# Background work paced by VectorE time, chains one step per block, and the centre tap of a short convolution on ACT

## The chip, the cores and the metric

One core of one Trainium2 chip. The metric is the device time of one execution in microseconds, lower is better. Engines are called PE (TensorE), DVE or VectorE, ACT (ScalarE), POOL (GpSimd) and SP (SyncE, which here only issues DMAs).

## The reference, cut to what matters

Two groups, each of 2048 tokens of width 1024, go through the same layer in float32:

```python
h = rmsnorm(x, norm_g)
p = h @ w_in                                   # 1024 -> 3328 columns
hy_u, hy_z, cf_a, cf_z, xa_q, xa_z = split(p)
k2   = hyena_two_sided_filter(...)             # 3 sine layers, times exp decay: (2L, 512)
u    = depthwise_conv(hy_u, width 3) + b;  x0, x1, v = split(u)
y_hy = x0 * bidir_fftconv(v * x1, k2, skip) * silu(hy_z)
y_cf = silu(layernorm(depthwise_conv(val * sigmoid(gate), width 31))) * silu(cf_z)
y_xa = memory_attention(xa_q, rmsnorm(mem), w_kv) * silu(xa_z)
x    = x + concat(y_hy, y_cf, y_xa) @ w_out;   y = rmsnorm(x)
```

## The kernel before

The run has four phases in time: the start (0 to 76 us), the projection `p = h @ w_in` (to about 1390), the FFT and attention stages (to about 1740) and the output projection. The change touches the projection only.

There the 3328 columns are cut into 26 tiles of 128, the tokens of a group into four blocks of 512 (`tb`). One **block** is one column tile for 512 tokens: `proj` (L402) issues 24 matmuls into one of two PSUM tiles "pj", three for each of eight k-steps, since every operand is split into a high and a low part (`split`, L176: a cast on ACT, a subtraction on POOL or VectorE). There are 104 blocks per group, 208 in all; I number them 1 to 208 in program order. The list `seq` (L632 to L641) sets the order of columns: conformer gate and value (cg, cv), conformer output gate (zc), the pairs x1 and v of the Hyena branch, the pairs of its gate zh and x0, and the attention's zx and q. The last entry of group 0 runs zx1 and q1 together, token block by token block (blocks 97 to 104), since each time group 0's x for a token block is done with, `build_xt` puts group 1's in its place.

After its matmuls a block has an epilogue. For x0, x1 and v that is `hy_conv` (L416): ACT copies the PSUM tile to SBUF (L423), POOL makes the centre tap with the bias (L430), VectorE adds the two outer taps (L432, L434), and `gate` multiplies on POOL (L451).

**Background work** is cut into steps kept in two queues, `bgq` and `fq`. After each block `background(BR, FR)` (L626) takes up to seven steps of `bgq` and one of `fq`, whatever they cost; not after blocks 97 to 104. What is in the queues, and after which column (`QUEUE`, L621; `n` counts columns of a group):

- `kv_background` (L523): keys and values of the memory, ten steps and two `store`s, taken at blocks 9 and 10.
- `cf_background(g)` (L209): the width-31 convolution and layer norm of the conformer, for four token blocks b. Each has two `start`s (a load and the first tap on POOL), 60 taps on VectorE (`tap`, L218) and then `center`, `var`, `norm`, `fin`, `outp`. `mean` (L223) adds two tiles on POOL, splits the sum and has PE add over channels by a matmul with ones (L227, L228). Group 0's is queued before block 25 and taken until block 63, group 1's is taken at blocks 125 to 163.
- `filter_background` (L271): the Hyena filter, 32 `taps` steps in eight groups b of four, each group after three `mlp` layers that follow on one another: a matmul (L294), then VectorE, POOL, VectorE, POOL, and a Sin on ACT (L305, L308). A `taps` step has three matmuls (L320 to L322), an Exp on ACT (L324), a product on VectorE (L325), a matmul with the Fourier matrix (L332), a copy on ACT (L333) and a store. It's queued at group 1's first column.
- `a_background` (L584): the first Fourier step of eight of the channels' pieces, queued late in group 1.

`load_x(1, tb)` (L369) brings in group 1's x, in two halves of 256 tokens: `normed` (L347) loads four pieces, each into a "bg" tile, for the sum of squares (L354), puts 1/rms on a diagonal in the first of these tiles (L363), spreads it over the partitions by two matmuls into an "ms" tile `r` (L364), and scales the half (L366). Then `build_xt` (L378) splits it (L385, L386). `load_x(1, 0)` is issued two columns before group 1, the other three inside the last entry of group 0.

**Tiles** are taken from pools by tag: "bg" has six (NBT; a conformer block holds four of them, `hb` and `acc` for two channels, and two more for the halves of each mean), "ms" is four PSUM tiles for all the background's matmuls and `r`, "big" three, "sm" six, "f512" two and "f256" three. A request waits until a tile is released. The order of instructions on each engine is laid out ahead of time from the program by a scheduler; work may stand earlier on its engine than where the program issues it. At the end `bg(len(bgq))` empties the queues.

Of the kernel before, what the change touches and what calls it, by code (L numbers as in the profile page):

```python
# [15 lines left out]
ALU = mybir.AluOpType  # L16
# [86 lines left out]
def kernel(ctx: ExitStack, tc: tile.TileContext, a: dict):  # L103
    nc = tc.nc
    LEAD, BR, FR, PF = 8, 7, 1.0, 0
# [53 lines left out]

    bgq, fq = deque(), deque()  # L160

    def bg(n, q=bgq):
        for _ in range(min(n, len(q))):
            q.popleft()()
# [23 lines left out]
    with ExitStack() as c1:  # L188
# [20 lines left out]
        def cf_background(g):  # L209
# [13 lines left out]
            def mean(src, tmp):  # L223
                mp, hi, lo = ms(), bt(TB, F32R), bt(TB, F32R)
                nc.gpsimd.tensor_tensor(tmp, src[0], src[1], op=ALU.add)
                split(hi, lo, tmp)
                nc.tensor.matmul(mp, ones, hi, start=True, stop=False)  # L227
                nc.tensor.matmul(mp, ones, lo, start=False, stop=True)  # L228
                return mp

            def center(st):
                mp = mean([st["a", c] for c in range(2)], st["h", 0][:, 0:TB])
                for c in range(2):
                    nc.vector.tensor_tensor(st["a", c], st["a", c], mp, op=ALU.subtract)

            def var(st):
# [3 lines left out]
                vp = mean([st["q", c] for c in range(2)], st["q", 1])  # L240
                nc.scalar.activation(st["q", 0], vp, AF.Sqrt, bias=eps)

            def norm(st):
                nc.vector.reciprocal(st["q", 0], st["q", 0])

            def fin(st, c):
                acc = st["a", c]
                nc.gpsimd.tensor_tensor(acc, acc, st["q", 0], op=ALU.mult)
                nc.scalar.activation(acc, acc, AF.Silu, bias=vb[:, 66 + c:67 + c], scale=vb[:, 64 + c:65 + c])

            def outp(st, b, c):
                z = st["q", 1 - c]
                nc.sync.dma_start(z, SZ[g][c][:, b * TB:(b + 1) * TB])
                acc = st["a", c]
                nc.gpsimd.tensor_tensor(acc, acc, z, op=ALU.mult)
                nc.sync.dma_start(YN[g][c][:, b * TB:(b + 1) * TB], acc)

            for b in range(NB):
                st = {}
                for c in range(2):  # L260
                    bgq.append(lambda st=st, b=b, c=c: start(st, b, c))
                for k in range(1, CK):
                    for c in range(2):
                        bgq.append(lambda st=st, c=c, k=k: tap(st, c, k))
                for f in (center, var, norm):
                    bgq.append(lambda st=st, f=f: f(st))
                bgq.append(lambda st=st, b=b: (fin(st, 0), fin(st, 1)))
                bgq.append(lambda st=st, b=b: (outp(st, b, 0), outp(st, b, 1)))


        def filter_background():  # L271
# [42 lines left out]
            def taps(st, b, n):  # L314
                n2p = b * 4 + n
                if n % 2 == 0:
                    st["tf"] = ft(W)
                    nc.sync.dma_start(st["tf"], a["tf"][:, n2p:n2p + 2, :].rearrange("p n k -> p (n k)"))
# [672 lines left out]
```

## Time and profile before

| | us |
|---|---|
| median of 3 runs | 2164.81 (2164.49 to 2169.85) |
| profiled execution | 2161.23 |
| its span | 2159.5 |
| PE busy in the span | 2009.7 (93%) |
| VectorE busy | 1297.8 (60%) |
| ACT busy | 807.3 (37%) |
| POOL busy | 1015.1 (47%) |
| mean granted TensorE clock | 0.978 |

PE works nearly all the time, so what isn't PE's work shows as a gap on PE or as a lower granted clock (1.00 stands for the upper of its two levels, 2.4 GHz, 0.50 for the lower, 1.2 GHz). The mean shares of the other engines hide that they differ by stretch: VectorE is over 90% busy in some and under 50% in others. So the profile is best read by stretches of the projection phase.

### The profile page before, as it was taken

To read this page: it belongs to the slowest core of one execution; us is meant where nothing else is said; L and a number is where in the kernel's file an instruction comes from. 1 tells how busy PE (TensorE), PEld (TensorE's weight loads), DVE (VectorE), ACT (ScalarE), POOL (GpSimd) and SP (SyncE) were. 2 spreads that over 40 slices of the span, in tenths; PEclk is the share of its full clock that TensorE was granted. 3 is DMA by queue.
4 is the path that set the end of the run, shared out by engine and by line. 5 is a ranking of instruction groups with operands and counts; after the bars stand their busy time and mean duration, and the time that the engine had idled before them with its cause. 6 is when DMAs were issued, how large, how long until landed. Compare 5 with 4: busy or idle time off the path is not lost.

```text
span 2159.5 us, 26758 instructions
## 1 busy us (share of the span) xinstructions
PE 2009.7 (93%) x9186; PEld 1604.0 (74%) x9186; DVE 1297.8 (60%) x1781; ACT 807.3 (37%) x1625; POOL 1015.1 (47%) x1015
## 2 busy tenths in 40 slices
PE   5999998898999999989989899999998889999998
PEld 5888876776787888877768687789732278888886
DVE  6664497977336473489494953287887724434443
ACT  5431212132524333322424244387787712111211
POOL 3434576576534323486565752364588811111110
PEclk9999999999999999999999999999999999999999
DMA  8541111121546222111212226798688785655552
GB/s 305 171 152 54 59 49 63 55 69 45 195 152 193 71 72 77 65 66 59 70 66 73 75 84 195 215 297 268 187 258 269 239 197 150 154 152 143 151 153 56
DMA packets 175842, 293.05 MB, mean 136 GB/s; under 512 B 50665, under 2 KB 71801, under 8 KB 172890
## 3 DMA queue, kind: packets, MB, share of 16 engines
q1 hardware_dynamic: 148474, 232.20, 35.3%
q10 hardware_dynamic: 21392, 46.18, 6.5%
q0 software_dynamic: 5840, 12.95, 2.2%
q8 instruction: 73, 1.20, 0.2%
q14 instruction: 63, 0.52, 0.1%
HBM read 186.87 MB, written 104.39 MB: 135 GB/s over the span
## 4 chain that ended last, share of the span: by engine, by line
PE 63%; DVE 16%; issue 6%; DMA 6%; POOL 4%; ACT 3%; SPq 1%; ACTq 0%; POOLq 0%; DVEq 0%
PE pj L410 11%; PE pj L409 11%; PE pj L411 11%; DVE bg L219 8%; PE ms L936 5%; PE ms L938 5%; PE ms L937 5%; PE tr L919 2%; PE po L760 2%; DVE sm L432 1%; DVE big L366 1%; DMA big<-in_xt_dram 1%; PE ms L739 1%; PE ms L332 1%; PE ms L546 1%
## 5 line engine op out<-in xcount | busy, mean ns | idle before, releaser
L409 PE MATMUL pj<-xh,whi 128*128 128x512 f32 (+1 forms) x1728 | 672.9, 390 | 24.2 <-ACT sm L423 6.6
L410 PE MATMUL pj<-xl,whi 128*128 128x512 f32 (+1 forms) x1728 | 671.6, 389 | 9.2 <-POOL xl L386 7.8
L411 PE MATMUL pj<-xh,wlo 128*128 128x512 f32 (+1 forms) x1728 | 670.4, 388 | 0.0
L219 DVE SCALAR_TENSOR_TENSOR bg<-bg,vb,bg 128x512 f32<-128x512 f32 x480 | 428.0, 924 | 10.7 <-POOL bg L214 5.9
L409 PEld LDWEIGHTS pj<-xh,whi 128*128 128x128 f32 x1728 | 332.0, 192 | 93.9 <-ACT sm L423 7.8
L410 PEld LDWEIGHTS pj<-xl,whi 128*128 128x128 f32 x1728 | 332.2, 192 | 74.1 <-POOL xl L386 8.7
L411 PEld LDWEIGHTS pj<-xh,wlo 128*128 128x128 f32 x1728 | 332.0, 192 | 64.6
L178 POOL TENSOR_TENSOR wlo<-sm,whi 128x256 fp32r<-128x256 f32 x204 | 190.5, 959 | 89.5 <-ACT whi L177 86.3
L936 PE MATMUL ms<-wo,mh 128*128 128x512 f32 x512 | 206.7, 404 | 1.8 <-ACT mh L177 1.8
L937 PE MATMUL ms<-wo,mh 128*128 128x512 f32 x512 | 201.3, 393 | 0.0
L938 PE MATMUL ms<-wo,ml 128*128 128x512 f32 x512 | 198.9, 395 | 0.2 <-POOL ml L178 0.2
L432 DVE SCALAR_TENSOR_TENSOR sm<-sm,va,sm 128x448 f32<-128x448 f32 (+1 forms) x96 | 82.7, 861 | 161.9 <-POOL sm L430 136.7
L939 DVE TENSOR_TENSOR xr<-xr,ms 128x512 f32<-128x512 f32 x64 | 44.0, 688 | 203.7 <-PE ms L938 203.7
L184 POOL TENSOR_TENSOR ss<-ss,mhalf 128x1 f32<-128x1 f32 x32 | 17.6, 550 | 315.9 <-DVE ss L183 315.9
L430 POOL TENSOR_SCALAR sm<-sm,va 128x448 f32<-128x448 f32 (+1 forms) x96 | 113.5, 1182 | 102.2 <-ACT sm L423 82.2
L451 POOL TENSOR_TENSOR big<-big,sm 128x448 f32<-128x448 f32 (+1 forms) x64 | 118.6, 1853 | 77.7 <-DVE sm L434 70.8
L182 ACT ACTIVATE junk<-xr 128x1024 bf16<-128x1024 f32 x32 | 33.8, 1058 | 318.4 <-DVE xr L939 318.2
L423 ACT COPY sm<-pj 128x512 f32<-128x512 f32 x96 | 56.0, 585 | 199.6 <-PE pj L411 150.1
L177 ACT CAST whi<-sm 128x256 fp32r<-128x256 f32 x208 | 73.0, 404 | 139.4 <-DMA sm<-in_win_dram 106.4
L936 PEld LDWEIGHTS ms<-wo,mh 128*128 128x128 f32 x512 | 97.2, 190 | 20.5 <-ACT mh L177 2.6
L938 PEld LDWEIGHTS ms<-wo,ml 128*128 128x128 f32 x512 | 96.4, 188 | 20.9 <-POOL ml L178 0.6
L937 PEld LDWEIGHTS ms<-wo,mh 128*128 128x128 f32 x512 | 97.2, 190 | 19.0
(179 smaller groups left out, 3096.9 us busy)
## 6 DMA issues: line engine op xcount, KB each, us to landing
sm<-in_win_dram SPq DMA_DIRECT2D x104, 256.0 KB, 3.4
big<-in_xt_dram SPq DMA_DIRECT2D x32, 512.0 KB, 5.9
in<-x1d SPq DMA_DIRECT2D x128, 128.0 KB, 3.3
aa<-o ACTq DMA_DIRECT2D x64, 256.0 KB, 3.6
at<-aa SPq DMA_DIRECT2D x64, 256.0 KB, 4.1
out_dram<-xr ACTq DMA_DIRECT2D x64, 256.0 KB, 3.3
x1d<-us ACTq DMA_DIRECT2D x48, 256.0 KB, 4.5
in<-xf SPq DMA_DIRECT2D x66, 128.0 KB, 3.7
```

Of the source, the lines that this page charges most:

```text
L177: nc.scalar.copy(hi, src)
L178: (sub_eng or nc.gpsimd).tensor_tensor(lo, src, hi.bitcast(F32), op=ALU.subtract)
L219: nc.vector.scalar_tensor_tensor(st["a", c], st["h", c][:, k:k + TB], vb[:, 2 * k + c:2 * k + c + 1], st["a", c], op0=ALU.mult, op1=ALU.add)
L409: nc.tensor.matmul(ps[:, ts_], hi, xh[:, k, ts_], start=k == 0, stop=False)
L410: nc.tensor.matmul(ps[:, ts_], hi, xl[:, k, ts_], start=False, stop=False)
L411: nc.tensor.matmul(ps[:, ts_], lo, xh[:, k, ts_], start=False, stop=k == KC - 1)
L430: nc.gpsimd.tensor_scalar(ct[:, o:e], pt[:, o + 1:e + 1], w[1], va[:, 52 + ch:53 + ch], op0=ALU.mult, op1=ALU.add)
L432: nc.vector.scalar_tensor_tensor(ct[:, o:e], pt[:, o:e], w[0], ct[:, o:e], op0=ALU.mult, op1=ALU.add)
L451: nc.gpsimd.tensor_tensor(v, v, out, op=ALU.mult)
L936: nc.tensor.matmul(po, mh[:, k, :], woh[k][:, hs], start=i == 0, stop=False)
L937: nc.tensor.matmul(po, mh[:, k, :], wol[k][:, hs], start=False, stop=False)
L938: nc.tensor.matmul(po, ml[:, k, :], woh[k][:, hs], start=False, stop=i == 7)
```

## The change

Each background step now carries a cost in us of VectorE and a flag "chain". After each block, `background(us)` gets a credit of 5.0 less the column's own VectorE cost (`own`: 2.2 for x0, x1 and v, 0.8 for cv and q, 0.1 for others) and takes steps while credit is left, `fq` before `bgq`, but at most one chain step of each queue per block. A tap costs 0.9 and is no chain step.

- The conformer's steps are cut anew: the sum and split of a mean stand at the end of one step, its matmul at the head of the next; per token block `start`, 60 taps, `total`, `center`, `var`, `outp`.
- The filter's `taps` loses its second half, which becomes `spec`, done one step later; a step is now `spec` of the tap step before, `taps`, and in 21 of 32 steps an `mlp` layer of the next group. It's queued at column 12 of group 0 (taken from block 57) instead of at group 1's first.
- `kv_background` and `a_background` are chain steps; the two `mult`s of an `a_background` piece become one step.
- In `hy_conv` the centre tap goes from POOL to ACT.

```diff
+    pace = {"block": 0, "credit": 0.0, "last": {id(bgq): -1, id(fq): -1}}
+    def background(us):
+        pace["block"] += 1
+        pace["credit"] = min(pace["credit"], us) + us
+        chained = set()
+        while pace["credit"] > 0:
+            for q in (fq, bgq):
+                if not q:
+                    continue
+                cost, chain, fn = q[0]
+                if chain and (id(q) in chained or pace["last"][id(q)] == pace["block"]):
+                    continue
+                if chain:
+                    chained.add(id(q))
+                q.popleft()
+                fn()
+                pace["last"][id(q)] = pace["block"]
+                pace["credit"] -= cost
+                break
+            else:
+                break
...
-            def mean(src, tmp):
-                mp, hi, lo = ms(), bt(TB, F32R), bt(TB, F32R)
+            def halves(st, src, tmp):
+                st["hi"], st["lo"] = bt(TB, F32R), bt(TB, F32R)
                 nc.gpsimd.tensor_tensor(tmp, src[0], src[1], op=ALU.add)
-                split(hi, lo, tmp)
...
+            def mean(st):
+                mp = ms()
+                nc.tensor.matmul(mp, ones, st["hi"], start=True, stop=False)
+                nc.tensor.matmul(mp, ones, st["lo"], start=False, stop=True)
...
+            def total(st):
+                halves(st, [st["a", c] for c in range(2)], st["h", 0][:, 0:TB])
...
-                for f in (center, var, norm):
-                    bgq.append(lambda st=st, f=f: f(st))
-                bgq.append(lambda st=st, b=b: (fin(st, 0), fin(st, 1)))
...
+                        bgq.append((0.9, False, lambda st=st, c=c, k=k: tap(st, c, k)))
+                bgq.append((0.5, True, lambda st=st: total(st)))
+                bgq.append((1.4, True, lambda st=st: center(st)))
+                bgq.append((3.4, True, lambda st=st: var(st)))
+                bgq.append((0.0, True, lambda st=st, b=b: (outp(st, b, 0), outp(st, b, 1))))
...
-            for b in range(8):
-                st = {}
-                for ly in range(3):
-                    fq.append(lambda st=st, b=b, ly=ly: mlp(st, b, ly))
-                for n in range(4):
-                    fq.append(lambda st=st, b=b, n=n: taps(st, b, n))
+            for ly in range(3):
+                fq.append((2.6, True, lambda ly=ly: mlp(st, 0, ly)))
+            for b in range(8):
+                for n in range(4):
+                    def step(b=b, n=n):
+                        if b or n:
+                            spec(b - (n == 0), (n - 1) % 4)
+                        taps(b, n)
+                        if b < 7 and n:
+                            mlp(st, b + 1, n - 1)
+                    fq.append((3.2 if b < 7 and n else 0.8, True, step))
+            fq.append((0.0, True, lambda: spec(7, 3)))
...
-            nc.gpsimd.tensor_scalar(ct[:, o:e], pt[:, o + 1:e + 1], w[1], va[:, 52 + ch:53 + ch],
-                                    op0=ALU.mult, op1=ALU.add)
+            nc.scalar.activation(ct[:, o:e], pt[:, o + 1:e + 1], AF.Identity, bias=va[:, 52 + ch:53 + ch], scale=w[1])
...
-        QUEUE = {(0, 0): [kv_background], (0, 4): [lambda: cf_background(0)], (1, 0): [filter_background],
+        QUEUE = {(0, 0): [kv_background], (0, 4): [lambda: cf_background(0)], (0, 12): [filter_background],
...
-                        background(BR * len(cs), FR)
+                        background(sum(5.0 - own(col) for col, _ in cs))
...
-        bg(len(fq), fq)
-        bg(len(bgq))
+        drain(fq)
+        drain(bgq)
```

## Rows read from the trace of the kernel before

**Rows 1.** busy us of each engine by stretch (start:end length), granted clock

```profile
core 0: us, PE busy (x) PEld busy (x) DVE busy (x) ACT busy (x) POOL busy (x), PEclk, DMA share, GB/s
76.00:1390.00 1314.00, 1239.76 (x5351) 1006.72 (x5350) 814.04 (x1025) 422.99 (x755) 677.98 (x705) 0.98 0.28 93
150.00:200.00 50.00, 50.00 (x222) 41.43 (x221) 32.28 (x45) 8.01 (x17) 18.70 (x12) 1.00 0.26 93
296.00:346.00 50.00, 36.95 (x147) 29.26 (x146) 45.43 (x51) 6.81 (x15) 34.15 (x31) 0.90 0.12 43
640.00:705.00 65.00, 60.79 (x277) 49.80 (x276) 42.51 (x87) 33.09 (x59) 32.31 (x22) 1.00 0.63 198
705.00:950.00 245.00, 245.00 (x1059) 198.69 (x1058) 125.93 (x164) 83.10 (x142) 102.81 (x138) 1.00 0.19 66
1210.00:1260.00 50.00, 41.61 (x157) 32.04 (x156) 48.04 (x59) 17.51 (x27) 23.41 (x23) 0.90 0.24 78
```

**Rows 2.** L219's instructions: ns min/median/max, first and last start

```profile
L219 DVE SCALAR_TENSOR_TENSOR bg<-bg,vb,bg x480: 652/749/2320, 131.4 to 1254.6; 128x512 f32<-128x512 f32 x160
```

**Rows 3.** PE's waits, two windows: total us, times, longest

```profile
PE ms L227 <- ACT bg L177: 22.4, 3, 9.1
PE pj L409 <- ACT sm L423: 5.7, 2, 3.4
...
PE ms L294 <- ACT f L305: 15.4, 4, 6.8
PE ms L332 <- DVE f L325: 7.4, 3, 3.9
```

**Rows 4.** costliest groups on the page: busy, mean ns | idle before

```profile
L430 POOL TENSOR_SCALAR sm<-sm,va 128x448 f32<-128x448 f32 (+1 forms) x96 | 113.5, 1182 | 102.2 <-ACT sm L423 82.2
...
L423 ACT COPY sm<-pj 128x512 f32<-128x512 f32 x96 | 56.0, 585 | 199.6 <-PE pj L411 150.1
```

**Rows 5.** groups of ACT's instructions by line, 80 to 1390 us

```profile
L249 ACT ACTIVATE bg<-bg,vb 128x512 f32<-128x512 f32 x16 | 13.1, 817 | 19.5 <-POOL bg L248 19.4
...
L305 ACT ACT_TABLE_LOAD x7 | 9.0, 1283 | 0.1
```

**Rows 6.** POOL in order of time: start us, us, line, operation

```profile
813.27 1.40 POOL L178 TENSOR_TENSOR bg<-bg,bg 128x512 fp32r<-128x512 f32 x1 [0.21 <-ACT bg L177]
```

**Rows 7.** PE in order of time, near 920 us

```profile
919.93 0.59 PE L294 MATMUL ms<-f,wf 128*128 128x256 f32 x2
920.18 0.58 PE L227 MATMUL ms<-bg,ones 128*128 128x512 f32 x1
```

**Rows 8.** ACT in order of time: Squares of four pieces of x

```profile
580.70 0.63 ACT L354 ACTIVATE bg<-bg 128x512 f32<-128x512 f32 x1 [1.15 <-DMA bg<-in_x_sample_dram]
...
590.99 0.63 ACT L354 ACTIVATE bg<-bg 128x512 f32<-128x512 f32 x1 [1.04 <-DMA bg<-in_x_sample_dram]
```

**Rows 9.** VectorE in order of time: end of a half's statistics

```profile
577.92 0.16 DVE L357 TENSOR_TENSOR ss<-acc 128x2 f32<-128x2 f32 x1 [8.14 <-ACT bg L354]
...
579.09 0.48 DVE L363 TENSOR_SCALAR bg<-ident,ss 128x128 f32<-128x128 f32 x2 [0.80 <-POOL ss L359]
```

**Rows 10.** PE in order of time: filter layers L294, then tap steps L320

```profile
785.78 0.60 PE L294 MATMUL ms<-f,wf 66*128 66x256 f32 x2
...
821.19 0.39 PE L320 MATMUL ms<-big 128*128 128x512 f32 x1
...
828.44 0.79 PE L320 MATMUL ms<-big 128*128 128x512 f32 x1
```

**Rows 11.** instructions of L366 and L385: ns min/median/max

```profile
L366 DVE SCALAR_TENSOR_TENSOR big<-big,va,ms x144: 472/476/483, 10.7 to 698.3; 128x256 f32<-128x256 f32 x144
...
L385 ACT CAST xh<-big x32: 1027/1042/1055, 12.8 to 698.8; 128x1024 fp32r<-128x1024 f32 x32
```

**Rows 12.** ACT in order of time, 850 to 857

```profile
852.87 1.28 ACT L305 ACT_TABLE_LOAD   x1
854.18 0.42 ACT L305 ACTIVATE f<-f 128x256 f32<-128x256 f32 x1
```

More of the change, by code (lines that the diff above doesn't have):

```diff
@@ L160, with drain @@
     bgq, fq = deque(), deque()
-    def bg(n, q=bgq):
-        for _ in range(min(n, len(q))):
-            q.popleft()()
+    pace = {"block": 0, "credit": 0.0, "last": {id(bgq): -1, id(fq): -1}}
[19 more added lines that the diff above has]
+                break
+    def drain(q):
+        while q:
+            q.popleft()[2]()
     def chans(d, g, n):
@@ L221, in tap @@
                     op0=ALU.mult, op1=ALU.add)
-            def mean(src, tmp):
-                mp, hi, lo = ms(), bt(TB, F32R), bt(TB, F32R)
+            def halves(st, src, tmp):
+                st["hi"], st["lo"] = bt(TB, F32R), bt(TB, F32R)
                 nc.gpsimd.tensor_tensor(tmp, src[0], src[1], op=ALU.add)
-                split(hi, lo, tmp)
-                nc.tensor.matmul(mp, ones, hi, start=True, stop=False)
-                nc.tensor.matmul(mp, ones, lo, start=False, stop=True)
-                return mp
+                split(st["hi"], st["lo"], tmp)
+            def mean(st):
+                mp = ms()
+                nc.tensor.matmul(mp, ones, st["hi"], start=True, stop=False)
+                nc.tensor.matmul(mp, ones, st["lo"], start=False, stop=True)
+                return mp
+            def total(st):
+                halves(st, [st["a", c] for c in range(2)], st["h", 0][:, 0:TB])
             def center(st):
-                mp = mean([st["a", c] for c in range(2)], st["h", 0][:, 0:TB])
+                mp = mean(st)
                 for c in range(2):
                     nc.vector.tensor_tensor(st["a", c], st["a", c], mp, op=ALU.subtract)
-            def var(st):
                 for c in range(2):
@@ L239, in var @@
                     nc.scalar.activation(st["q", c], st["a", c], AF.Square)
-                vp = mean([st["q", c] for c in range(2)], st["q", 1])
+                halves(st, [st["q", c] for c in range(2)], st["q", 1])
+            def var(st):
+                vp = mean(st)
                 nc.scalar.activation(st["q", 0], vp, AF.Sqrt, bias=eps)
-            def norm(st):
                 nc.vector.reciprocal(st["q", 0], st["q", 0])
[L246 to L249, printed above, removed]
+                for c in range(2):
+                    nc.gpsimd.tensor_tensor(st["a", c], st["a", c], st["q", 0], op=ALU.mult)
             def outp(st, b, c):
@@ L254, in outp @@
                 acc = st["a", c]
+                nc.scalar.activation(acc, acc, AF.Silu, bias=vb[:, 66 + c:67 + c], scale=vb[:, 64 + c:65 + c])
                 nc.gpsimd.tensor_tensor(acc, acc, z, op=ALU.mult)
@@ L259, in cf_background @@
                 st = {}
[L260 to L261 removed]
+                bgq.append((0.0, False, lambda st=st, b=b: (start(st, b, 0), start(st, b, 1))))
                 for k in range(1, CK):
                     for c in range(2):
[L264 to L268 removed]
+                        bgq.append((0.9, False, lambda st=st, c=c, k=k: tap(st, c, k)))
[3 more added lines that the diff above has]
+                bgq.append((0.0, True, lambda st=st, b=b: (outp(st, b, 0), outp(st, b, 1))))
         def filter_background():
```

44 lines of the change are left out of this document (23 added, 21 removed).

## The prediction

> **What bounds the kernel now.** I read the slices of the page first (PE at nine or ten tenths nearly everywhere), then the busy time by stretch. The projection phase, 76 to 1390 us, has 1239.76 us of PE work in 1314 us at a mean granted clock of 0.98 [rows 1]: 74 us idle and about 0.02 x 1314 = 26 us given up to the lower of the two clock levels, 100 us in all. It isn't spread evenly. From 150 to 200 us PE is never idle and a block costs 24 x 50 / 222 = 5.41 us (5.44 over longer stretches); from 705 to 950, with the filter and the short convolutions beside it and VectorE busy for only 125.93 us, 245 of 245 us are busy. The loss sits where VectorE is full: 296 to 346 (PE 36.95 of 50, VectorE 45.43, clock 0.90) and 1210 to 1260 (41.61, 48.04, 0.90) [rows 1]. Of six such stretches these are the first and the last (between them lie 396 to 446, 500 to 556, 950 to 1035 and 1095 to 1145). The six together have 63 us of idle PE and 31 us of lower clock: **94 us**. The clock there falls after PE has stood still; where PE never stands still it's 1.00.
>
> The cause is arithmetic. Before, seven steps are taken per block; a tap's median is 749 ns [rows 2], so 5.2 us of VectorE per block, and the change itself puts the column's own work at up to 2.2: 7.4 us against 5.4 of PE. What then ends PE's waits: the conformer's mean matmul L227 (22.4 us in 3), a short convolution that gives back its PSUM tile late, and the filter's L294 and L332 behind ACT and VectorE [rows 3].
>
> **The change, part by part.** All sums are made against the profiled execution, 2161.2 us (span 2159.5); the median of the three runs is 3.6 above it.
>
> *Pacing.* A block's credit is 5.0 minus the column's own VectorE cost, so 2.8 in x0, x1 and v blocks: about 3 taps at 0.9, that is 3 x 0.75 + 2.2 = 4.5 us of VectorE in 5.4 us of PE. The queue empties just in time (I walked it block by block: the last conformer block of group 1 ends at block 199 of 208). So the overload should go, and chains move one step per block, so that a mean matmul is issued blocks after its input. Upper end: all 94 us; I see nothing by which it would cost time in itself but for the last rival. Lower end: the waits that have nothing to do with taps stay, 5.7 + 15.4 + 7.4 = 28.5 us [rows 3], with the lower clock in proportion 28.5 x 94/63 = 42, which leaves a gain of 52. I take **-78** (16 left), nearer to the upper end since the stretch from 705 to 950 runs the same filter chain without a stall [rows 1].
>
> *Centre tap on ACT.* It removes 96 POOL operations of 1182 ns, 113.5 us, and adds 96 to ACT. Bounds for one: 585 ns, the plain copy of the same tile [rows 4], to 817, an ACT operation from SBUF with scale and bias [rows 5]: 56 to 78 us. If it needed a table load each time, 96 x 1.283 = 123 more [rows 5]. ACT is busy 8.01 of 50 us without background [rows 1], so it's covered, and PE's tile is freed by the copy before it: **0**, and less on POOL doesn't shorten PE's path. Behind it in ACT's queue stand the next block's copy out of PSUM and the filter's activations; where those fill ACT, the cover is gone (third rival).
>
> *The key-value work one step per block*, blocks 9 to 20 instead of 9 and 10: same work, PE does it anyway, its tiles are free by block 25: 0.
>
> *The group switch.* This is the part that decides. `load_x(1, ...)` brings the second group's input through the "bg" tag, 32 pieces of one tile each, issued after blocks 95, 98, 100 and 102. Before, the conformer of group 0 is done by block 63 and all six tiles are free. After, the third conformer block of group 0 starts at block 73, is starved by the filter (which is asked first), and holds four of six tiles until block 109: its `total` asks for two more only at block 106, behind the 32 pieces. That tiles of a tag are given out in the order of the program the trace bears out: the conformer's mean matmul had its input at 813.27 + 1.40 us, yet ran at 920.18, right behind the filter's L294 at 919.93 that was issued before it [rows 6, 7] (four of four such cases agree). So eight halves of x go through two tiles, one of them kept for the half's diagonal until its L364. With one tile to move through, pieces came at 580.70 to 590.99, three gaps of 3.43 us [rows 8], and the end of a half, statistics to diagonal, is 577.92 to 579.57, 1.65 [rows 9], about 2.3 with the matmul: 3 x 3.45 + 2.3 = 12.65 us per half.
>
> Each half's `r` needs an "ms" tile as well, and by the same order stands behind the filter's last. The filter is programmed for blocks 57 to 94, one step per block. But three layers took 821.19 - 785.78 = 35.4 us, 11.8 each, and a tap step 6.8 [rows 10]. I take 10.5 a layer: 3 x 10.5 + 7 x (3 x 10.5 + 6.8) + 4 x 6.8 = 327 us; PE gets through its 47 blocks up to 104 in 47 x 5.44 + 65 of background (36 filter steps of some 1.6 us of PE, and the means) = 321. So the filter ends when group 0 ends, not at block 94. From the first `r` the eighth is 7 x 12.65 = 88.6 us later; with the scaling of a half (8 x 0.476) and the split into high and low (3.7: two casts of 1.04 and the subtraction behind) [rows 11] 96. PE has three blocks, 16.3 us, to do meanwhile: it waits 80, plus 8 for a filter that ends after block 104, less the 4.2 us that it idles there now [rows 1]: **+84**. Bounds: +25 if the filter ends at block 94 (the halves then start 55 us earlier), +105 if a layer keeps its 11.8.
>
> *The tail.* Eight steps of `a_background` are left after block 208 and are drained behind the last projection: four matmul steps, three transposes and a load of some 1 to 3 us each, partly beside the next stage: **+7** (0 to 15). *The clock* after PE has stood still at the switch: **+3** (0 to 10), since PE's clock in the windows above was 0.90 with 8 to 13 us idle in 50 [rows 1].
>
> Sum: 2161.2 - 78 + 0 + 84 + 7 + 3 = **2177**; own range of this case 2145 to 2207.
>
> **Rivals.**
> - *The filter keeps its programme* (0.18). If a layer takes one block (6.8 us, as a tap step does [rows 10]) and not two, the filter ends at block 94, PE waits only 25 us at the switch, and 2161.2 - 78 + 25 + 7 + 3 = 2118: faster. The point from which it decides: with the switch costing less than about 68 us the change isn't slower. For it: VectorE is no longer full when the filter runs. Against: the 11.8 us come from a stretch where PE and VectorE weren't waiting either [rows 1, 10].
> - *The pieces don't wait* (0.14). If the tiles are given out otherwise, the conformer finishes first or the pieces find tiles: 2161.2 - 78 + 7 = 2090. Against it stand [rows 6, 7].
> - *ACT becomes the bound in the gate columns* (0.10). The fused step puts Exp (taps) and Sin (next layer) into every step; each change costs a load of 1.283 [rows 5]; 21 fused steps make about 26 loads more, 33 us of ACT. A gate block gives ACT a Silu, copies, weight casts, Exp, Sin and two or three loads, and the block beside it the centre tap. If two thirds of one load per fused step find no cover, PE loses 21 x 1.283 x 2/3 = 18 on top of the sum: 2195. The load is followed at once by the next activation, 852.87 + 1.28, then 854.18 [rows 12]. The Trainium skill, "ScalarE: Activation LUTs", section "What ACT_TABLE_LOAD costs", states 1283 ns and a drain of about 1380 more for every switch of sets; estimated by its 2.66 us the 26 switches would be 69 us of ACT. The row shows the load and no drain, so the trace agrees with half of it.
> - *The pacing doesn't act on what the scheduler lays out* (0.10). The taps of the first conformer block, issued from block 25, started at 131.4 us [rows 2], blocks before their place, so work is packed ahead wherever VectorE looks free. If half of the gain is lost so, 39 instead of 78: 2216.
>
> **How the numbers follow.** The forecast has 0.48, the rivals 0.18, 0.14, 0.10, 0.10. A measurement can tell about 0.3% from no change, 6.5 us: 2158 to 2171 is "same". Faster: both faster rivals (0.32) and 0.07 of the forecast's lower end; same: 0.10, all from the forecast's range; slower: 0.31 of it and 0.20 of the rivals. The range must take in the second rival in part and reaches to the fourth: 2092 to 2214.
>
> **What would show it.** Right: PE without idle stretches from 250 to 560 us and in group 1, VectorE under 45 of 50 there; then, at the group switch, one gap row after another, PE's L409 or L364 waiting, with Squares L354 every 3.4 us and the last L332 of the filter shortly before the first L364. Wrong: Squares L354 four at a time; or the filter's L332 ending well before the last blocks of group 0; or PE gaps in the gate columns with ACT as releaser; or a tail after the last projection of more than 15 us.

## The result, and the profile after

The changed kernel is slower: 2264.1 us (median of 4 runs, 2254.9 to 2266.0) against 2167.3 for the kernel before; the ratio is 1.0437, with a 95% interval of 1.0407 to 1.0467. The forecast was 2177 with a range that ended at 2214. The profiled execution has a span of 2260.7 us, 101.2 more than before. Line numbers below are those of each kernel's own file; in the changed kernel `proj`'s matmuls are L449 to L451, a tap is L244, the copy out of PSUM L463, the centre tap L470, the edge columns L462, the outer taps L471 and L473, `r` L404, a Square of a piece of x L394, and the filter's lines L321 (layer), L349 to L351 and L365 (last matmul of a step).

Cut at the same blocks, the two spans differ so:

| stretch | before | after | difference |
|---|---|---|---|
| start to block 103 | 688.3 | 701.1 | +12.8 (the filter's matmuls came in here, some 43 us; idle time and lower clock fell by 30) |
| blocks 104 to 107, the group switch | 22.5 | 166.6 | **+144.1** |
| blocks 108 to 208 | 677.6 | 601.4 | -76.2 (the filter's matmuls left) |
| behind the projection | 771.1 | 791.6 | +20.5 |

So away from the switch the projection gained 63.4 us, the switch lost 144.1, and the next stage 20.5. The busy time by stretch of the changed kernel (start:end, length, busy us and instructions of each engine, granted clock), cut at blocks 25, 57, 97, 104, 108, 125, 161, 197 and at the end of the projection, of which blocks 97 to 103, 108 to 124 and 197 to 208 are left out; behind it, the kernel before in blocks 25 to 56, 57 to 96, 125 to 160 and 161 to 196:

```profile
core 0: us, PE busy (x) PEld busy (x) DVE busy (x) ACT busy (x) POOL busy (x), PEclk, DMA share, GB/s
197.00:378.00 181.00, 177.11 (x773) 145.73 (x772) 115.80 (x135) 60.17 (x103) 83.32 (x89) 0.99 0.16 52
378.00:655.40 277.40, 262.31 (x1097) 207.11 (x1098) 155.35 (x208) 148.06 (x221) 133.63 (x159) 0.98 0.27 91
701.10:867.70 166.60, 67.53 (x181) 42.02 (x179) 56.35 (x124) 64.58 (x115) 34.70 (x39) 0.64 0.36 116
967.70:1176.30 208.60, 199.62 (x870) 163.96 (x869) 164.75 (x186) 66.26 (x115) 122.63 (x109) 0.98 0.18 60
1176.30:1395.10 218.80, 203.16 (x873) 165.60 (x872) 150.11 (x160) 68.67 (x108) 136.82 (x93) 0.97 0.22 69
1469.10:2260.70 791.60, 733.37 (x3546) 559.31 (x3544) 435.11 (x653) 343.53 (x772) 312.21 (x287) 0.97 0.69 194
```

```profile
196.90:390.50 193.60, 180.55 (x778) 148.05 (x778) 134.70 (x138) 42.76 (x81) 124.09 (x127) 0.97 0.17 57
390.50:643.20 252.70, 230.42 (x986) 188.34 (x984) 153.80 (x190) 74.17 (x148) 134.42 (x128) 0.95 0.31 102
811.90:1050.10 238.20, 226.16 (x950) 180.83 (x949) 149.19 (x176) 72.75 (x132) 139.12 (x171) 0.98 0.19 65
1050.10:1296.40 246.30, 228.44 (x952) 183.00 (x951) 178.44 (x211) 99.31 (x149) 145.03 (x147) 0.97 0.22 77
```

In the switch PE is busy 67.5 of 166.6 us at a granted clock of 0.64. [rows 1] show the same place before, 640 to 705, with 4.2 us idle at 1.00. PE's longest wait there (total us, times, longest), and PE in order of time at the filter's end:

```profile
PE ms L404 <- DVE bg L403: 56.1, 6, 14.9
```

```profile
758.57 1.13 PE L365 MATMUL ms<-f,f 128*128 128x512 f32 x2 [0.84 <-DVE f L354]
759.54 0.61 PE L404 MATMUL ms<-bg,ones 128*128 128x128 f32 x4
775.03 1.20 PE L404 MATMUL ms<-bg,ones 128*128 128x128 f32 x4 [14.89 <-DVE bg L403]
```

The first `r` (L404) stands right behind the filter's last matmul, 758.57, and the next comes 15.5 us later, after 14.89 us idle. Eight halves end with an `r` at 863.3, so (863.3 - 759.5) / 7 = 14.8 us each. Group 0's last matmul had ended at 708.0.

### The profile page after: what moved, and what is told of

Read it like the earlier page. It is cut to its first block, busy times and chain, and to the rows that moved or that the text cites. A ratio compares the mean times of both kernels' runs of the same rounds, so it can differ in the third digit from the quotient of the medians.

```text
span 2260.7 us, 26846 instructions
## 1 busy us (share of the span) xinstructions
PE 2031.4 (90%) x9186; PEld 1609.7 (71%) x9186; DVE 1271.2 (56%) x1781; ACT 908.2 (40%) x1739; POOL 960.7 (42%) x919
## 4 chain that ended last, share of the span: by engine, by line
PE 60%; DVE 14%; DMA 8%; issue 7%; POOL 5%; ACT 4%; SPq 1%; POOLq 0%; ACTq 0%; DVEq 0%
PE pj L449 10%; PE pj L450 10%; PE pj L451 10%; DVE bg L244 9%; PE ms L973 5%; PE ms L975 5%; PE ms L974 5%; PE tr L956 2%; PE po L797 2%; DMA bg<-in_x_sample_dram 1%; PE tr L791 1%; PE ms L776 1%; PE ms L365 1%; DMA sm<-in_win_dram 1%; POOL big L490 1%
## 5 line engine op out<-in xcount | busy, mean ns | idle before, releaser
L449 PE MATMUL pj<-xh,whi 128*128 128x512 f32 (+1 forms) x1728 | 675.3, 391 | 63.9 <-ACT sm L463 22.8
L451 PE MATMUL pj<-xh,wlo 128*128 128x512 f32 (+1 forms) x1728 | 669.5, 388 | 0.0
L449 PEld LDWEIGHTS pj<-xh,whi 128*128 128x128 f32 x1728 | 331.9, 192 | 139.0 <-ACT sm L463 26.7
L244 DVE SCALAR_TENSOR_TENSOR bg<-bg,vb,bg 128x512 f32<-128x512 f32 x480 | 413.8, 908 | 3.5 <-POOL bg L239 0.7
L451 PEld LDWEIGHTS pj<-xh,wlo 128*128 128x128 f32 x1728 | 331.4, 192 | 65.6 <-issue 0.7
L203 POOL TENSOR_TENSOR wlo<-sm,whi 128x256 fp32r<-128x256 f32 x204 | 190.7, 959 | 99.1 <-ACT whi L202 96.7
L471 DVE SCALAR_TENSOR_TENSOR sm<-sm,va,sm 128x448 f32<-128x448 f32 (+1 forms) x96 | 85.1, 886 | 147.7 <-ACT sm L470 146.2
L490 POOL TENSOR_TENSOR big<-big,sm 128x448 f32<-128x448 f32 (+1 forms) x64 | 124.6, 1947 | 77.9 <-DVE sm L473 77.7
L463 ACT COPY sm<-pj 128x512 f32<-128x512 f32 x96 | 56.2, 586 | 176.3 <-PE pj L451 156.1
L202 ACT CAST whi<-sm 128x256 fp32r<-128x256 f32 x208 | 72.6, 402 | 119.3 <-DMA sm<-in_win_dram 98.5
L462 POOL TENSOR_SCALAR sm<-sm 128x65 f32<-128x65 f32 x72 | 74.2, 1032 | 96.1 <-ACT sm L463 72.2
L470 ACT ACTIVATE sm<-sm,va 128x448 f32<-128x448 f32 (+1 forms) x96 | 78.3, 816 | 89.3 <-POOL sm L462 68.7
L973 PEld LDWEIGHTS ms<-wo,mh 128*128 128x128 f32 x512 | 97.5, 191 | 21.1 <-ACT mh L202 3.0
```

The source lines that it names most:

```text
L203: (sub_eng or nc.gpsimd).tensor_tensor(lo, src, hi.bitcast(F32), op=ALU.subtract)
L244: nc.vector.scalar_tensor_tensor(st["a", c], st["h", c][:, k:k + TB], vb[:, 2 * k + c:2 * k + c + 1], st["a", c], op0=ALU.mult, op1=ALU.add)
L449: nc.tensor.matmul(ps[:, ts_], hi, xh[:, k, ts_], start=k == 0, stop=False)
L451: nc.tensor.matmul(ps[:, ts_], lo, xh[:, k, ts_], start=False, stop=k == KC - 1)
L462: nc.gpsimd.tensor_scalar(pt[:, 0:65], st["p"][:, 512:577], 1.0, 0.0, op0=ALU.mult, op1=ALU.add)
L470: nc.scalar.activation(ct[:, o:e], pt[:, o + 1:e + 1], AF.Identity, bias=va[:, 52 + ch:53 + ch], scale=w[1])
```

## The experiments

For all runs below the measure away from the switch is PE's idle time and the lower clock in four stretches, blocks 25 to 56, 57 to 96, 125 to 160 and 161 to 196, worked out from the trace as for the table above (idle is length less busy; clock is the time that the lower level cost, half of the time spent at it). Idle time at the lower level stands in both columns, some 14 to 16 us of it in the kernel before and in the changed one, so only differences between rows are read. Each row is one profiled execution:

| kernel | idle, four stretches | sum | lower clock | both |
|---|---|---|---|---|
| before | 13.1, 22.3, 12.0, 17.9 | 65.3 | 30.6 | **95.9** |
| changed | 3.9, 15.1, 9.0, 15.6 | 43.6 | 17.1 | **60.7** |
| changed, centre tap on POOL | 5.1, 18.8, 17.0, 18.6 | 59.4 | 25.6 | 85.0 |
| before, centre tap on ACT | 8.6, 19.4, 6.6, 13.1 | 47.7 | 23.8 | 71.5 |
| the same, POOL operation put back | 11.1, 24.5, 10.4, 18.0 | 64.0 | 28.9 | 92.9 |
| changed, edge columns on ACT | 9.0, 8.8, 7.2, 15.2 | 40.2 | 17.0 | 57.2 |
| before, four steps per block | 10.1, 16.4, 5.4, 9.2 | 41.2 | 22.2 | 63.4 |
| the same, taps tied | 12.6, 28.2, 41.7, 32.4 | 114.9 | 64.9 | 179.8 |
| changed, taps tied | 1.4, 18.9, 0.0, 2.3 | 22.6 | 15.4 | **38.0** |
| all repairs | 1.4, 18.0, 0.0, 2.3 | 21.7 | 10.2 | **31.9** |

**The group switch.** The pieces of group 1's x from other tiles, then `r` from another tag, then both:

```diff
-                sq.append(bt())
+                sq.append(sm() if own else bt())
...
-            r = ms()[:, 0:256]
+            r = (tr() if own else ms())[:, 0:256]
```

Pieces in "sm" tiles:

> The changed kernel, but the 32 pieces of group 1's x use tiles of the tag sm instead of bg. In the profile of the changed kernel the stretch from the last matmuls of block 104 to block 108 takes 166.6 us (701.1 to 867.7), against 22.5 in the kernel before. Theory (two shortages in a row): the filter's last L365 at 758.6 holds back every r, and then the halves come 14.8 us apart because two bg tiles must do. Here only the second shortage goes: the first r still stands right behind the filter's last matmul, and the halves then come about 7 us apart (a load of 512 KB takes 5.0, the scaling 3.2), so about 60 us less: 2264 - 60 = 2205. Rival (the halves are slow because of their loads, not their tiles): the halves stay 13 to 15 us apart and the time stays near 2260.

Measured 2212.4, some 7 above the expected. The first `r` still ran at 753.5, 0.4 us behind the filter's last L365, but three more halves had their `r` within 1.4 us, so tiles were what had kept the pieces apart. Blocks 97 to 107 took 163.7 us (changed kernel 212.3, before 67.6).

`r` in a "tr" tile:

> The changed kernel, but r of group 1's halves is taken from the PSUM tag tr instead of ms; the pieces stay in bg. Theory: the first r no longer waits for the filter's end and runs some 100 us earlier, around 650; the halves still come about 14.8 us apart, so the eighth is there at about 650 + 7 x 14.8 = 755, some 50 us behind the last block of group 0, of which 16 are covered by blocks of group 1 and some by the filter's own matmuls: 2264 - 100 = 2165 (2150 to 2190). Rival (the order of ms tiles isn't what holds r back): first r still behind the filter's last matmul, near 2260.

Measured 2200.8. The first `r` ran at 646.9, 112 us before; so what held it was the wait for an "ms" tile behind the filter. But the halves came 20 us apart, not 14.8, the eighth at 789.8 instead of 755, and blocks 97 to 107 still took 138.3.

Both:

> Both edits at once: pieces of group 1's x in sm tiles, r in a tr tile. Theory: the group switch costs about what it costs in the kernel before (22.5 us for the same stretch; up to 25 more, as the filter still holds one of three big tiles), so 2264 - 144 + 10 = 2130, and faster than the kernel before by some 35 us, since outside the switch the changed kernel gained 63 us and lost 20 in the first part of the next stage. Rival (the filter, moved into group 0, is itself what makes the switch late, through PE time or VectorE): 2200 or more.

Measured 2189.1, ratio to the kernel before 1.0115 (1.0091 to 1.0140): 75 us better than the changed kernel, but 59 short of the expectation, and not faster than before. Blocks 97 to 107 took 115.5, 97 less than in the changed kernel and 48 more than before, of which 19 are matmuls of the filter; PE idled 25.5 us there, against 99.1 in the changed kernel and 4.2 before. Blocks 125 to 160 lost 19 us more. The two shortages are the cause of two thirds of the switch's price; the rest stayed open here.

The filter put back where the kernel before queues it:

```diff
-        QUEUE = {(0, 0): [kv_background], (0, 4): [lambda: cf_background(0)], (0, 12): [filter_background],
+        QUEUE = {(0, 0): [kv_background], (0, 4): [lambda: cf_background(0)], (1, 0): [filter_background],
...
-                        bgq.append((0.9, False, lambda st=st, c=c, k=k: tap(st, c, k)))
+                        bgq.append((0.8, False, lambda st=st, c=c, k=k: tap(st, c, k)))
```

> The changed kernel with the filter queued where the kernel before has it, at group 1's first column, and the price of a tap lowered from 0.9 to 0.8 so that the conformer of group 0 is done before group 1's x is loaded (program place: block 94). Theory: all six bg tiles are free at the switch and no filter stands before r, so the switch costs what it did before (22.5 us): 2264 - 144 = 2120, plus some 5 to 10 for more left-over steps at the end (14 instead of 8), 2125 to 2135. Rival (pacing itself loses, through chains issued late): 2180 or more, with the loss spread over the projection.

Measured 2162.7, level with the kernel before (0.9991, 0.9968 to 1.0014), and some 30 over the expectation. The switch was mended, 33.0 us for blocks 104 to 107. But in this profile, which is of the slowest of ten executions (2181.4), blocks 161 to 196 lost 53.7 us, with 28 taps of one conformer block in block 188, and the part behind the projection took 808.7 us, 37.6 more than before, for 14 left-over steps. So pacing without the switch's price doesn't win either. The next question was what the pacing itself does.

**The centre tap alone**, which I had put at nothing:

> The kernel before with the centre tap of the short convolution on ACT and nothing else. Theory (off PE's path): within 0.3% of the kernel before, 2160 to 2171; POOL's busy time falls by some 113 us and ACT's rises by about 78. Rival: the shorter way from the PSUM copy to the outer taps lets VectorE run earlier and saves 10 us or more; second rival: an activation in front of the next copy out of PSUM holds PE and costs 10 or more.

Measured 2144.7 against 2167.6, ratio 0.9906 (0.9870 to 0.9941): the first rival, a gain of 22.9 us. And back on POOL in the changed kernel:

> The changed kernel with the centre tap back on POOL. Theory (off PE's path, the loss is the group switch): within 0.5% of the changed kernel, 2253 to 2275. Rival (ACT in the filter's layers is late because of the 96 more activations): the filter ends earlier and the time falls by 20 us or more.

Measured 2283.8, 19.7 more than the changed kernel: my theory's "within 0.5%" fails the same way. By the table the centre tap takes 24 us out of the losses in either kernel, and the pacing with all its moves only 95.9 - 85.0 = 10.9. (The profiled execution behind the 85.0 was 10 us slower than the median of its kernel; by the medians the centre tap is worth 19.7 and the pacing up to some 16.) Why the centre tap gains, one run tells in the main: an operation that computes nothing new is put back on POOL, behind the outer taps.

```diff
             nc.vector.scalar_tensor_tensor(out, rows(pt[:, o + 2:e + 2]), w[2], rows(ct[:, o:e]),
                                            op0=ALU.mult, op1=ALU.add)
+            nc.gpsimd.tensor_scalar(pt[:, 65:512], pt[:, 65:512], 1.0, 0.0, op0=ALU.mult, op1=ALU.add)
```

> The kernel before with the centre tap on ACT, and an operation on POOL put back that computes nothing new: behind the outer taps it reads and rewrites 447 columns of the short convolution's input with the same values, 96 times. It tells apart why the centre tap on ACT gains 20 us. Theory (POOL's operations on SBUF slow VectorE's taps down, and their number is what counts): the gain is lost, 2160 to 2170. Rival (the way from the PSUM copy to the outer taps got shorter): the gain stays, 2140 to 2150.

Measured 2160.2, ratio 0.9975 (0.9961 to 0.9988): 5 us of the 22.9 are left. Most of the gain came from POOL having less to do, not from a shorter chain. The conformer's taps bear out that VectorE pays for POOL's work: they took 924 ns on average before, 901 with the centre tap on ACT, and 926 with the operation put back. (The operation also holds its tile a little longer and stands in POOL's queue ahead of the gate's product; that part isn't told apart.)

**What POOL and VectorE do to each other.** POOL and VectorE of the changed kernel in order of time (start, duration):

```profile
1341.09 23.05 POOL L203 TENSOR_TENSOR big<-big,big 128x512 fp32r<-128x512 f32 x1 [5.69 <-ACT big L202]
```

```profile
1349.78 8.04 DVE L244 SCALAR_TENSOR_TENSOR bg<-bg,vb,bg 128x512 f32<-128x512 f32 x12
...
1365.23 1.04 DVE L471 SCALAR_TENSOR_TENSOR sm<-sm,va,sm 128x512 f32<-128x512 f32 x1 [2.25 <-ACT sm L470]
...
1368.48 5.80 DVE L244 SCALAR_TENSOR_TENSOR bg<-bg,vb,bg 128x512 f32<-128x512 f32 x4
```

A subtraction of 128x512 on POOL, 1.27 to 1.83 us in the 27 others of its line and size in the projection, took 23.05. VectorE ran taps and outer taps without a gap from 1332.97 to 1362.98, the twelve shown in 8.04 us, 0.67 each. VectorE then paused for the 2.25 us before 1365.23, and POOL's operation ended in that pause, at 1364.1. Where POOL gets through, at 1368.48, four taps take 5.80, 1.45 each. The Trainium skill, "SBUF — State Buffer", section "SBUF: two separate sides", says that the two engines share a port pair, that an instruction of VectorE with two SBUF inputs and one of POOL that reads SBUF exclude each other, and that the loser fully blocks. The trace agrees, and goes further than "for the whole instruction": POOL lost against a whole run of taps. The forecast has no term for it.

A copy of 65 columns (L462) on POOL stands between the PSUM copy and ACT's centre tap, so I took it for what holds PE (the two columns of zeros at the ends move to ACT with it):

```diff
...
-                nc.gpsimd.tensor_scalar(pt[:, 0:65], st["p"][:, 512:577], 1.0, 0.0, op0=ALU.mult, op1=ALU.add)
+                nc.scalar.copy(pt[:, 0:65], st["p"][:, 512:577])
...
```

> The changed kernel with the edge columns of a short convolution (72 copies of 65 columns and the zero columns) moved from POOL to ACT; the rest as in the changed kernel. There one such copy of 65 columns on POOL took 7.02 us (1114.45 to 1121.43) while VectorE ran taps without a gap, and 12.05 at most, against 0.24 at least; ACT's centre tap waited for it (68.7 us in 17 waits), and PE behind ACT. Theory (POOL, starved by runs of taps, is what holds up PE outside the group switch): the 60 us of idle PE and lower clock in blocks 25 to 96 and 125 to 208 fall below 35, so 2264 - 30 = 2234 (2220 to 2245). Rival (VectorE's own backlog holds the PSUM tiles): no change, 2255 to 2275.

> The kernel before with the centre tap and the edge columns of the short convolution on ACT; its queues, places and rates are untouched. Theory (POOL was in PE's path, pacing is not needed): of the 100 us of idle PE and lower clock in the projection of the kernel before the centre tap alone brought 23; with the edge columns gone too another 15 to 30 go: 2167 - 23 - 22 = 2122 (2110 to 2135). Rival (the rest is VectorE's overload, which only pacing can take away): as with the centre tap alone, 2140 to 2150.

Measured 2258.5 (5.6 less than the changed kernel) and 2157.2 (2147.1 to 2164.8; no better than with the centre tap alone, and above the rival's range of 2140 to 2150). Both theories fail: moving that copy only moves the blockade, as the split of the weights on POOL went from 975 to 1201 ns on average in the changed kernel. This suggests that it isn't one operation that must leave POOL, but the runs of taps that must go.

**Does the pacing pace?** One conformer block's 60 taps (block 1 of group 1) in the changed kernel and, below, in the version with tied taps; the columns are length, VectorE busy (instructions of this line) and clock:

```profile
1080.00:1154.40 74.40, 50.33 (x60) 0.95 0.18 64
```

```profile
1064.00:1162.00 98.00, 61.55 (x60) 1.00 0.17 60
```

Sixty in 74.4 us and sixty in 98.0. By program they are due in blocks 143 to 161, at most six in a block. In the changed kernel they ran in blocks 145 to 156, up to nine in a block, and with tied taps in blocks 145 to 162, up to six. In all eight conformer blocks the scheduler laid the changed kernel's taps out in ten to twelve blocks, where by the credits they have between 11 and 33. A first try with a lower rate:

```diff
-    LEAD, BR, FR, PF = 8, 7, 1.0, 0
+    LEAD, BR, FR, PF = 8, 4, 1.0, 0
```

> The kernel before with four background steps per block instead of seven; nothing else. Theory (the place a step is issued at doesn't set when it runs, since the scheduler lays out ahead of time how early a tap may stand on VectorE): taps still come five to ten per block in runs of some twelve blocks, and the time is within 15 us of the kernel before, 2150 to 2180. Rival (pacing acts): no more than four or five taps per block, and the 100 us lost in the projection fall to about 40: 2105 to 2120.

Neither as expected: 2197.1. The four stretches lose 63.4 instead of 95.9, so a lower rate does help, while taps still came up to 14 in a block. But the last conformer block's 60 taps all fell into block 199, with PE waiting 52.1 us for one mean, and blocks 197 to 208 took 148.1 us instead of 92.0.

Then a tie that binds: a block's first tap adds to its accumulators a zero that ACT makes from that block's PSUM tile.

```diff
...
+                        tie["z"] = tiny.tile([P, 1], F32, tag="tie", name=nm("tie"))
+                        nc.scalar.activation(tie["z"], ps[:, 0:1], AF.Copy, scale=0.0)
...
+                if st.get("blk") != tie["n"]:
+                    st["blk"] = tie["n"]
+                    for j in range(2):
+                        nc.vector.tensor_tensor(st["a", j][:, 0:1], st["a", j][:, 0:1], tie["z"], op=ALU.add)
```

> The kernel before with four background steps per block, as in the run before it, and now each block's taps are tied to that block: the first tap of a block adds a zero column to its two accumulators, and the zero is made on ACT from the block's own PSUM tile (one more 128x1 operation on ACT and two on VectorE per block). With four steps per block alone, blocks 25 to 196 lost 63 us in idle PE and lower clock, with up to 14 taps in a block. Theory (what loses time is that the scheduler lays taps out in dense runs, and a pace that binds would end it): at most four or five taps per block, and blocks 25 to 196 lose less than 30; the time falls by some 35 us plus what blocks 197 to 208 recover. Rival (VectorE is short in these blocks however the taps are spread): the 63 us stay.

> The kernel before with the centre tap on ACT, four background steps per block and tied taps. Theory (binding pace and the centre tap add up): from 2145 with the centre tap alone another 30 us: 2115 (2100 to 2130). Rival (they take away the same stalls): 2135 to 2150.

Measured 2227.1 and 2189.6 (ratio 1.0110): both theories fail. With the old queues a bound pace makes it worse, 179.8 us lost in the four stretches. There filter and conformer stand in the same blocks of group 1, up to 13 taps still come in one block, and PE waits for the tie itself (27.8 us in three waits in group 0); which of these costs most was not tried. In the changed kernel's queues, with credits by VectorE time, it's another thing:

> The changed kernel with taps tied to the block they are issued behind, and nothing else: the group switch and the end of the projection are as in the changed kernel. Theory: blocks 25 to 56 and 125 to 196, where the changed kernel loses 37.8 us and the version with all repairs lost 3.7, lose under 6 here; the switch keeps its price (98.6 idle and 54.5 of lower clock in blocks 104 to 107): 2264 - 34 = 2230 (2215 to 2245). Rival (the tie helped only together with the mended switch): 2255 or more.

Measured 2214.5, 50 us less than the changed kernel. Busy time by stretch, blocks 25 to 56, 104 to 107, 125 to 160 and 161 to 196:

```profile
198.60:375.90 177.30, 175.90 (x776) 145.28 (x775) 150.91 (x212) 63.05 (x136) 83.21 (x95) 1.00 0.16 53
711.70:852.30 140.60, 55.78 (x156) 37.00 (x154) 52.84 (x114) 53.96 (x102) 30.97 (x30) 0.63 0.39 127
953.20:1150.10 196.90, 196.90 (x869) 162.94 (x868) 173.16 (x243) 68.97 (x149) 95.90 (x105) 1.00 0.18 62
1150.10:1352.40 202.30, 199.95 (x874) 164.76 (x873) 170.96 (x223) 70.50 (x144) 104.69 (x95) 0.99 0.23 74
```

From block 125 to 160 PE is never idle, at full clock; 12.4 us were lost there. The three stretches without filter lost 40.4 in the changed kernel (the expectation's 37.8 is too low) and lose 5.4; blocks 57 to 96, with the filter, lose 32.6 instead of 20.2. The longest of the 65-column copies on POOL fell from 12.05 us to 1.45:

```profile
L462 POOL TENSOR_SCALAR sm<-sm x72: 239/640/12054, 203.4 to 1372.1; 128x65 f32<-128x65 f32 x72
```

```profile
L467 POOL TENSOR_SCALAR sm<-sm x72: 244/684/1451, 205.0 to 1332.9; 128x65 f32<-128x65 f32 x72
```

The median stayed; the tie ended the long blockade. Whether its gain comes by that or by outer taps that wait for fewer conformer taps on VectorE isn't told apart. The tie was worth more than expected since the switch became 26 us shorter too: the filter ended 17 us earlier, and group 0 some 11 us later.

**The end of the projection.** `a_background`'s steps without the chain flag:

```diff
-                bgq.append((0.7, True, lambda i=i: trans(i)))
-                bgq.append((0.7, True, lambda i=i: (mult(i, 0), mult(i, 1))))
+                bgq.append((0.7, False, lambda i=i: trans(i)))
+                bgq.append((0.7, False, lambda i=i: (mult(i, 0), mult(i, 1))))
```

> The changed kernel with the steps of a_background not marked as chain steps, so that all of them are issued before block 208 and none is left to be drained. Theory: the stretch behind the projection, 791.6 us in the changed kernel and 771.1 in the kernel before, goes back to about 772, and the projection is some 10 us longer by the same matmuls: 2264 - 10 = 2254 (2245 to 2260). Rival (the first part of the next stage is late for another reason, as the last stores of the projection): 2260 or more, with the same 790 us behind the projection.

Measured 2253.6, as expected, with 770.4 us behind the projection instead of 791.6.

**All repairs together** (pieces, `r`, end of the projection, tied taps):

> The changed kernel with the group switch mended (pieces of x in sm tiles, r in a tr tile), the steps of a_background not marked as chain steps, and taps tied to the block they are issued behind, as in the other run of this call. With the switch mended alone it took 2189. Theory (pacing didn't bind; with a binding pace the 60 us that the changed kernel still loses in blocks 25 to 96 and 125 to 208 fall to about 25, and the stretch behind the projection falls by 10): 2189 - 10 - 35 = 2144 (2130 to 2160), faster than the kernel before. Rival: 2170 or more, with the same losses in these blocks.

Measured 2134.4, ratio to the kernel before 0.9863 (0.9843 to 0.9883): faster than both kernels, 130 us less than the changed one. Behind the projection it takes 769.7 us. Blocks 97 to 107 and blocks 125 to 160:

```profile
663.60:773.70 110.10, 86.06 (x336) 66.53 (x335) 75.88 (x152) 73.85 (x137) 45.11 (x47) 0.86 0.66 213
874.00:1071.40 197.40, 197.40 (x872) 163.33 (x871) 179.51 (x243) 72.18 (x152) 99.54 (x106) 1.00 0.18 64
```

What is left is the filter's stretch (blocks 57 to 96 lose 28 us) and the switch, 110.1 us where the kernel before took 67.6; 16.5 of them are matmuls of the filter, and 24.0 are idle. To see whether the idle time comes from the filter's late end (its last matmul ran at 787.9), the filter is queued earlier:

```diff
-        QUEUE = {(0, 0): [kv_background], (0, 4): [lambda: cf_background(0)], (0, 12): [filter_background],
+        QUEUE = {(0, 0): [kv_background], (0, 4): [lambda: cf_background(0)], (0, 8): [filter_background],
```

> All repairs (pieces of x in sm tiles, r in a tr tile, no chain steps at the end, tied taps), and the filter queued at column 8 of group 0 instead of column 12, so that by program it ends at block 77 instead of 94. Theory (what the mended switch still costs, 28 us idle and 15 of lower clock in blocks 97 to 107, is the filter's end at 766 us and the big tile it holds): with the filter ended by about 680 the switch costs 10 us: 2134 - 30 = 2104 (2095 to 2120). Rival (the price comes from the x pieces themselves): 2125 to 2140.

Measured 2157.9, worse by 23.5. The filter ended at 658 us and the switch took 98.5 us, 11.6 less; but blocks 57 to 96 now lost 64.0 us. PE still idled 25.7 us in the switch: what got shorter is the filter's own share. So the filter's end isn't what makes PE wait in the mended switch. In both kernels PE waits there for the diagonal of a half (9.9 us at most with all repairs, 8.9 with the filter queued earlier), and with all repairs the eight `r` come 13 us apart, 671.8 to 763.5, where in the kernel before they took 42.7 us in all. That the halves' loading sets this is read from the trace and was not tried.

## Why the prediction was wrong

**Where the profile was right.** The stretches that lose time, the cause of the switch's price (four of six "bg" tiles held, `r` behind the filter's last "ms" tile) and the filter's end behind group 0 came as written; the signs named for the switch are in the trace (PE waits for `r`'s diagonal, the Squares come one at a time, 3.7 us apart on average, and the filter's last matmul stands right before the first `r`). That gave the right sign, and 2177 for 2264. The sign named for the pacing isn't there: VectorE was still busy 49.8 of 50 us from 1220 to 1270.

**The pacing term (-78).** This is the step that failed first. The sum took the program's place of a tap for the time it runs; [rows 2] spoke against it, and I had it as the fourth rival at a chance of 0.10. The losses in the four stretches fell by 10.9, from 95.9 to 85.0, by pacing and all its moves without the centre tap (up to some 16 by the medians). The scheduler laid taps out in dense runs as before, until a tie made the place bind; with it the change's own queues lose 38.0, of which 5.4 away from the filter. So the price per block fits there, and nothing enforced it.

**The centre tap (0).** Measured -22.9 in the kernel before and -19.7 in the changed one. The error was to ask only whose path POOL is on. POOL's work costs VectorE time, as the taps' 924, 901 and 926 ns above show, and VectorE was full exactly there. The step to mistrust is "less on POOL doesn't shorten PE's path". [rows 4] show 1182 ns on average for an operation that takes 704 at least, 823 in the median and 7671 at most:

```profile
L430 POOL TENSOR_SCALAR sm<-sm,va x96: 704/823/7671, 203.4 to 1274.4; 128x512 f32<-128x512 f32 x48, 128x448 f32<-128x448 f32 x24, 128x576 f32<-128x576 f32 x24
```

Something held it up, and that wasn't asked after: the longest of them, from 479.0 us, ran beside eleven taps that followed one another without a gap.

**The group switch (+84, and +3 for the clock).** Measured +144.1. Two sizes were off. The filter took 758.6 - 389.1 = 369.5 us from its first layer and not 327, since the first three layers took 437.0 - 389.1 = 47.9 us instead of 31.5 and a group of three layers and four tap steps 46 on average (437.0 to 713.3 for six) instead of 38.3. It ended some 51 us behind group 0's last matmul at 708.0, where 8 stood in the sum: +43. A half took 14.8 us, not 12.65: 7 x 2.15 = +15. Together that is 58, and 144 is 57 more than the 87 of the sum. (One reading was loose: the two tap steps of [rows 10] are 7.25 us apart; 6.8 is the distance of the next ones.)

**The tail (+7).** Measured +20.5, beyond its bound of 15; PE idled 15.0 us in the first 61.6 us behind the projection (3.6 before). The run without chain steps gives it back. The left-over steps are a serial chain at a place where nothing covers it; I priced them as covered in part.

**The rivals and the range.** The two faster rivals (0.32) both stood on the pacing term; with the 35 us that the four stretches gave instead of 78 they come to 2161 and 2133. The fourth rival's mechanism was the right one, but it was added to a switch term that was itself too low. The measured terms add up to 2161.2 - 11 - 24 + 144 + 20 = 2290, against 2262.5 for this execution. Of the 28 between, 18 are blocks 197 to 208 (92.0 before, 74.0 after): filter matmuls that now run earlier, `a_background` steps that now lie behind the projection, and 4 us of idle time. The other 10 fit the 50 of the filter's 208 matmuls that ran inside the switch, 30.0 us busy: its price counts that time, and group 1 no longer has the work. The third rival's sign (a gap in the gate columns, blocks 57 to 88, with ACT as releaser) is there once: PE waited 9.3 us, to 404.4, for the Silu of a gate block. But ACT wasn't full. It had idled 12.75 us before the cast of a conformer sum that stood ahead of that Silu and waited for POOL and the taps, and blocks 57 to 96 as a whole lost less than before.

## What to carry to other kernels

Where a scheduler lays the instructions out, the place at which the program issues background work is no pace; check in the trace in which blocks it really ran, and if a pace matters, make it a dependence on the block's own result. Before a consumer of a tile tag is moved in the program, list who else takes tiles of that tag (PSUM tags too) between its old place and its new one: the requests are served in program order, and what is held across the point where another user needs many costs the whole wait. An operation on POOL that is on nobody's path may still be paid for by VectorE; here the sign of it was a mean far above the median.

## What was not expected of the hardware

One POOL operation of 128x512 took 23.05 us and one of 128x65 took 12.05 while VectorE ran taps with two SBUF inputs back to back, against 1.27 and 0.24 at the shortest. The first ended 1.15 us into VectorE's first pause. The second ended at 1261.01, 0.07 us after the only break that the trace shows in a run of 33 taps, one of 0.035 us before the tap that started at 1260.94; that tap took 1.33 us. Ninety-six operations of 447 columns on POOL, put back behind the chain, cost the kernel 15.5 us (2160.2 against 2144.7).
